# A decoder layer on one core: 3 of 8 pairs of k-tiles of the second SwiGLU's up-projections as 2x2 Strassen products

## The chip, the core and the metric

The kernel runs on one core of one Trainium2 chip. A core has a matrix engine (TensorE, PE in the rows), a vector engine (VectorE, DVE), a scalar engine (ScalarE, ACT), GpSimd (POOL) and SyncE (SP), which here issues the DMAs. Each engine works through its own list of instructions in order and waits at semaphores for the others. SBUF holds operands; products of PE go to PSUM, eight banks of 128 x 512 float32. The metric is the device time of one execution in microseconds (us); lower is better.

## What is computed

One layer with 256 tokens and a model width of 2048. This change concerns the second half-step alone, with `D_FF` = 5632:

```python
def swiglu(x, w1, w3, w2):
    return (jax.nn.silu(x @ w1) * (x @ w3)) @ w2

def reference(x, ...):
    h = x
    h = h + 0.5 * swiglu(rmsnorm(h, ffn1_norm[l]), ffn1_w1[l], ffn1_w3[l], ffn1_w2[l])
    ...                                             # attention and S5 mixers
    h = h + jnp.concatenate([a, s], axis=-1) @ w_out[l]
    h = h + 0.5 * swiglu(rmsnorm(h, ffn2_norm[l]), ffn2_w1[l], ffn2_w3[l], ffn2_w2[l])
    return rmsnorm(h, final_norm)
```

All is float32 and is compared as such. The kernel gets float32 accuracy from PE by splitting each operand into a high part (rounded to the type `fp32r`) and a low part, and by three passes for each product: high x high, high x low, low x high.

## The kernel before

**Tiles.** Tokens are two tiles of 128 (`NT` = 2, index `tt` or `t`), the 2048 channels are 16 k-tiles of 128, taken in 8 pairs. `Norm.cols` (L213) transposes four k-tiles of h on PE into two PSUM banks of the tag "tp" and splits them into `xh` and `xl`, the left operands of all later products; it is called once for each 512 columns of h at the end of the output projection, and `Norm.rstd` then works out the row scale in small DVE instructions.

**Half-step.** `ffn` (L248) goes over 11 chunks of 512 columns. For each, `gemm_rows` (L165) makes x @ w1 for both token tiles into two banks of the tag "mm", ACT takes Silu (L298), `gemm_rows` makes x @ w3 into two more, and DVE multiplies (L302). The gates are transposed (L313, into "tp" banks) and split into the left operand of the product with w2. That product, `down`, is delayed by one chunk: half of the previous chunk's `down` runs between a chunk's up-projections and its transposes, the other half behind the transposes; the first chunk has none before it. Its results are added into h by DVE (L258).

**Weights.** `wload` (L145) has SP load two k-tiles x 512 columns (512 KB) into one of five `raw` slots. `wtiles` (L153) splits each load: `whi` by ACT (L123), `wlo` by DVE (L124), each 128x1024, into one of three slots. A slot is free again when PE's last pass that reads it is done. Each such weight pair serves 2 k-tiles x 2 token tiles x 3 passes = 12 instructions of PE (L176 to L178).

**PSUM.** Tag "mm" has four banks, "tp" two (transposes), "sd" two (the S5 and attention parts, unused in the half-steps).

**Order.** The framework's scheduler sets each engine's list from program order and priorities: the splits of weights are raised by 50 places (`tc.high_priority(offset=50)`), so they stand ahead of other work on ACT and DVE. All other tiles come from one pool of 48 slots of 2 KB, `work`, called wk in rows.

## Time and profile before

| | before |
|---|---|
| median of three runs (lowest to highest) | 1852.6 us (1851.58 to 1853.11) |
| the profiled execution: its own time | 1852.75 us |
| its span, first to last instruction | 1850.2 us |
| PE busy | 1826.3 us, 99% |
| DVE busy | 1196.9 us, 65% |
| ACT busy | 834.2 us, 45% |
| GpSimd busy | 14.7 us |
| loaded from memory | 337.16 MB |
| granted PE clock, mean share of full speed | 0.999 |

Busy times count an instruction from its start to its end; consecutive instructions of an engine overlap somewhat, so starts in a timeline tell more of the pace than durations. Rows of the kernel before carry its line numbers; rows of the order below marked "now" carry those of the changed kernel, where `split` is L127 (ACT) and L128 (DVE).

### The profile page before, as it was taken

What the parts mean: (1) busy time and instruction counts of PE and PEld (TensorE: products, weight loads), DVE (VectorE), ACT (ScalarE), POOL (GpSimd) and SP (SyncE); (2) the same over time, 40 slices, a digit from 0 to 9 for tenths busy, and PEclk for the clock granted to TensorE, in tenths of its full rate; (3) what the DMA queues carried; (4) which work ended last, traced back from release to release, by engine and by line L of the source; (5) the groups of instructions that cost most, each with busy time, mean ns of one, the idle gap of its engine ahead of it and who ended that gap; (6) DMA issues with size and microseconds to landing.
All of it is one profiled execution on the core that took longest, in us unless ns stands there. A gap on an engine that the chain in (4) does not pass through costs nothing.

```text
span 1850.2 us, 24247 instructions
## 1 busy us (share of the span) xinstructions
PE 1826.3 (99%) x9365; PEld 1530.0 (83%) x9365; DVE 1196.9 (65%) x1636; ACT 834.2 (45%) x1081; POOL 14.7 (1%) x32
## 2 busy tenths in 40 slices
PE   8999999999999999999999999999999999999997
PEld 6888888888888888999987788888888888888886
DVE  5477667787887456789876565556555556555656
ACT  6444444434444444555437654443444444444444
POOL 0000000000000000000000000000000000000002
PEclk9999999999999999999999999999999999999999
DMA  7676666665666665654663467666666666666663
GB/s 241 188 210 193 188 188 189 187 177 176 182 198 190 193 187 190 170 149 141 183 211 113 128 180 215 189 188 192 193 189 188 193 192 189 188 193 193 188 194 130
DMA packets 193286, 340.84 MB, mean 184 GB/s; under 512 B 21034, under 2 KB 30868, under 8 KB 193172
## 3 DMA queue, kind: packets, MB, share of 16 engines
q1 hardware_dynamic: 193172, 339.31, 61.4%
q8 instruction: 73, 1.20, 0.3%
q14 instruction: 41, 0.34, 0.0%
HBM read 337.16 MB, written 2.11 MB: 183 GB/s over the span
## 4 chain that ended last, share of the span: by engine, by line
PE 52%; DVE 3%; issue 1%; DMA 1%; ACT 0%; ACTq 0%; SPq 0%; DVEq 0%
PE mm L176 14%; PE mm L178 14%; PE mm L177 14%; PE mm L187 1%; PE mm L188 1%; PE mm L189 1%; PE sd L634 1%; DVE wlo L124 1%; PE tp L798 1%; PE sd L822 1%; PE tp L313 1%; DVE wk L646 0%; PE tp L661 0%; DMA raw<-in_w_in_dram 0%; PE tp L819 0%
## 5 line engine op out<-in xcount | busy, mean ns | idle before, releaser
L124 DVE SCALAR_TENSOR_TENSOR wlo<-raw,whi 128x1024 fp32r<-128x1024 f32 (+1 forms) x620 | 759.1, 1225 | 577.2 <-ACT whi L123 576.1
L123 ACT ACTIVATE whi<-raw 128x1024 fp32r<-128x1024 f32 (+1 forms) x620 | 658.0, 1061 | 922.1 <-PE mm L178 814.5
L176 PE MATMUL mm<-whi,xh 128*128 128x512 f32 x1536 | 601.4, 392 | 2.0 <-ACT whi L123 2.0
L177 PE MATMUL mm<-wlo,xh 128*128 128x512 f32 x1536 | 600.1, 391 | 0.0
L178 PE MATMUL mm<-whi,xl 128*128 128x512 f32 x1536 | 599.8, 391 | 0.0
L176 PEld LDWEIGHTS mm<-whi,xh 128*128 128x128 f32 x1536 | 288.7, 188 | 62.0 <-ACT whi L123 2.4
L177 PEld LDWEIGHTS mm<-wlo,xh 128*128 128x128 f32 x1536 | 288.8, 188 | 60.2 <-DVE wlo L124 1.1
L178 PEld LDWEIGHTS mm<-whi,xl 128*128 128x128 f32 x1536 | 288.6, 188 | 59.5 <-DVE xl L124 0.4
L176 PE MATMUL mm<-whi,wk 128*128 128x512 f32 x688 | 270.3, 393 | 0.0
L178 PE MATMUL mm<-whi,wk 128*128 128x512 f32 x688 | 268.4, 390 | 0.0
L177 PE MATMUL mm<-wlo,wk 128*128 128x512 f32 x688 | 268.0, 390 | 0.0
L178 PEld LDWEIGHTS mm<-whi,wk 128*128 128x128 f32 x688 | 129.1, 188 | 27.1
L176 PEld LDWEIGHTS mm<-whi,wk 128*128 128x128 f32 x688 | 129.2, 188 | 26.6 <-issue 0.6
L177 PEld LDWEIGHTS mm<-wlo,wk 128*128 128x128 f32 x688 | 129.3, 188 | 26.0
L258 DVE SCALAR_TENSOR_TENSOR h<-mm,h 128x512 f32<-128x512 f32 x176 | 113.5, 683 | 2.8 <-PE mm L270 2.1
L187 PE MATMUL mm<-xh,whi 128*128 128x256 f32 x384 | 112.7, 294 | 0.9 <-DVE wk L882 0.9
L188 PE MATMUL mm<-xh,wlo 128*128 128x256 f32 x384 | 108.8, 283 | 0.0
L189 PE MATMUL mm<-xl,whi 128*128 128x256 f32 x384 | 108.8, 283 | 0.0
L187 PEld LDWEIGHTS mm<-xh,whi 128*128 128x128 f32 x384 | 73.4, 191 | 2.8 <-issue 1.2
L188 PEld LDWEIGHTS mm<-xh,wlo 128*128 128x128 f32 x384 | 73.4, 191 | 0.7 <-issue 0.2
L189 PEld LDWEIGHTS mm<-xl,whi 128*128 128x128 f32 x384 | 73.3, 191 | 0.4 <-issue 0.4
L298 ACT ACTIVATE wk<-mm,rstd 128x512 f32<-128x512 f32 x44 | 30.0, 681 | 20.0 <-PE mm L178 20.0
(246 smaller groups left out, 999.7 us busy)
## 6 DMA issues: line engine op xcount, KB each, us to landing
raw<-in_ffn_w_dram SPq DMA_DIRECT2D x528, 512.0 KB, 3.7
raw<-in_w_in_dram SPq DMA_DIRECT2D x48, 512.0 KB, 3.7
raw<-in_w_out_dram SPq DMA_DIRECT2D x32, 512.0 KB, 3.6
raw<-in_w_in_dram SPq DMA_DIRECT2D x8, 536.0 KB, 4.1
raw<-in_glu_w_dram SPq DMA_DIRECT2D x8, 512.0 KB, 4.7
h<-in_x_dram SPq DMA_DIRECT2D x4, 512.0 KB, 8.1
raw<-in_cmp_w_k_dram SPq DMA_DIRECT2D x4, 512.0 KB, 4.5
raw<-in_cmp_w_v_dram SPq DMA_DIRECT2D x4, 512.0 KB, 6.8
```

The costliest lines, as they stand in the source:

```text
L123: S.activation(hi, src, AF.Copy if isinstance(scale, float) else AF.Identity, scale=scale)
L124: V.scalar_tensor_tensor(lo, src, scale, hi.bitcast(F32), op0=ALU.mult, op1=ALU.subtract)
L176: PE.matmul(o, xh[:, t], hi[:, i, :n], start=kt == k0, stop=False)
L177: PE.matmul(o, xh[:, t], lo[:, i, :n], start=False, stop=False)
L178: PE.matmul(o, xl[:, t], hi[:, i, :n], start=False, stop=kt == k1 - 1)
L187: PE.matmul(o, wh, xh, start=kt == 0 and q % 2 == 0, stop=False, skip_group_check=True)
L188: PE.matmul(o, wl, xh, start=False, stop=False, skip_group_check=True)
L189: PE.matmul(o, wh, xl, start=False, stop=last, skip_group_check=True)
L258: V.scalar_tensor_tensor(o, p, 0.5, o, op0=ALU.mult, op1=ALU.add)
L298: S.activation(sl, ps1[tt], AF.Silu, scale=rstd[:, tt:tt + 1])
L313: PE.transpose(ps[:, k, tt * 128:tt * 128 + 128], gates[tt][:, f:f + 128], ident)
L634: PE.matmul(ps[:, hf * 256:hf * 256 + 256], s5.bt[i // 2][ri][:, 2 * (i % 2) + hf, :], up[:, hf].rearrange("p a c -> p (a c)"), start=True ...
```

## The change

In the second half-step alone, w1 and w3 of a chunk are treated as one right operand. For a pair of k-tiles the product is then 2x2 tiles (2 token tiles x 2 k-tiles) by 2x2 tiles (2 k-tiles x {w1, w3}), eight tile products with three passes each. For pairs 1, 3 and 5 (`WINO`) it is made by Strassen's method in Winograd's form, from seven products of sums:

- The four sums of left tiles are made once, in `Norm.combine` at the end of the output projection, and kept.
- The four sums of weight tiles are made for each chunk by DVE from the raw weights (L318), and each sum is split by ACT and DVE into `work` tiles, as is the second k-tile of w3.
- The seven products go to banks of their own: m1, m5, m6, m7 (the four "mm" banks), m2 and m3 ("tp"), m4 and e ("sd"). The three converted pairs accumulate in the same banks. The five other pairs keep eight products, which accumulate straight into m2, m3, m4 and e, the banks that end up as the four results.
- After pair 5, ACT and DVE begin the recombination (L335 to L339), and after pair 7 they add the rest and make the gates.

The body of the loop in `ffn` calls `up_wino` in place of the two `gemm_rows`; `down`, the transposes and the pools stay.

```diff
+WINO = (1, 3, 5)
...
+        def combine(self, pair, ps, scales):
+            y, s = work([128, 2, T]), work([128, 4, 128])
+            for k in range(2):
+                S.activation(y[:, k, :], ps[:, k, :], AF.Identity, scale=scales[k])
+            a11, a21, a12, a22 = (y[:, k, t * 128:t * 128 + 128] for k in range(2) for t in range(NT))
+            V.tensor_tensor(s[:, 0, :], a21, a22, ALU.subtract)
+            V.tensor_tensor(s[:, 2, :], a11, a21, ALU.subtract)
+            V.tensor_tensor(s[:, 1, :], s[:, 0, :], a11, ALU.subtract)
+            V.tensor_tensor(s[:, 3, :], a12, s[:, 1, :], ALU.add)
+            sh, sl = work([128, 4, 128], F32R), work([128, 4, 128], F32R)
+            split(sh, sl, s)
+            self.wino[pair] = sh, sl
...
+        def up_wino(c):
+            m1, m5, m6, m7 = (mm_tile() for _ in range(4))
+            m2, m3 = tp_tile(), tp_tile()
+            m4, e = sd_tile(), sd_tile()
...
+            for p in range(KT // 2):
+                raw1, raw3 = (wload(w[p * 256:p * 256 + 256, f], 512)[:, :, :512] for w in (w1, w3))
+                end = p == KT // 2 - 1
+                if p not in wino:
+                    with tc.high_priority(offset=50):
+                        ws = wpair(raw1), wpair(raw3)
+                    for k in range(2):
+                        for (hi, lo), os in zip(ws, ((m2, m4), (m3, e))):
+                            for t, o in enumerate(os):
+                                passes(o, *pure(k, 2 * p + k, t), hi[:, k, :], lo[:, k, :], end and k == 1)
+                    continue
+                done_ = p == max(wino)
+                with tc.high_priority(offset=50):
+                    hi, lo = wpair(raw1)
+                    b22 = work([128, 512], F32R), work([128, 512], F32R)
+                    split(*b22, raw3[:, 1, :])
+                    sums = []
+                    for a, b in ((raw1[:, 0, :], raw3[:, 0, :]), (0, raw3[:, 1, :]), (raw3[:, 0, :], raw3[:, 1, :]), (1, raw1[:, 1, :])):
+                        s = work([128, 512])
+                        V.tensor_tensor(s, sums[a] if isinstance(a, int) else a, b, ALU.add)
+                        sums.append(s)
+                    sw = []
+                    for s in sums:
+                        sw.append((work([128, 512], F32R), work([128, 512], F32R)))
+                        split(*sw[-1], s)
+                ah, al = xs.wino[p]
+                left = [(ah[:, i, :], al[:, i, :]) for i in range(4)]
+                passes(m1, *pure(0, 2 * p, 0), hi[:, 0, :], lo[:, 0, :], done_)
+                passes(m2, *pure(1, 2 * p + 1, 0), hi[:, 1, :], lo[:, 1, :], False)
+                passes(m3, *left[3], *b22, False)
+                passes(m5, *left[0], *sw[0], done_)
+                passes(m6, *left[1], *sw[1], done_)
+                passes(m7, *left[2], *sw[2], done_)
+                passes(m4, *pure(1, 2 * p + 1, 1), *sw[3], False)
+                if done_:
+                    u1, u2, u3, v, w = (work([128, 512]) for _ in range(5))
+                    S.activation(u1, m1, AF.Copy)
+                    V.tensor_tensor(u2, m6, u1, ALU.add)
+                    V.tensor_tensor(u3, m7, u2, ALU.add)
+                    V.tensor_tensor(v, m5, u2, ALU.subtract)
+                    V.tensor_tensor(w, m5, u3, ALU.subtract)
+            gates = []
+            for t, (a, ua, b, ub) in enumerate(((m2, u1, m3, v), (m4, u3, e, w))):
+                V.tensor_tensor(ua, a, ua, ALU.add)
+                sl = work([128, 512])
+                S.activation(sl, ua, AF.Silu, scale=rstd[:, t:t + 1])
+                V.tensor_tensor(ub, b, ub, ALU.add)
+                V.scalar_tensor_tensor(sl, ub, rstd[:, t:t + 1], sl, op0=ALU.mult, op1=ALU.mult)
+                gates.append(sl)
+            return gates
...
-                n2.cols(n)
+                n2.cols(n, WINO)
...
-    ffn(ffn2_w1[0], ffn2_w3[0], ffn2_w2[0], n2, n2.rstd(), finish, by_tokens=True)
+    ffn(ffn2_w1[0], ffn2_w3[0], ffn2_w2[0], n2, n2.rstd(), finish, by_tokens=True, wino=WINO)
```

Three places show what the change does to the lists of instructions. The names in rows are tiles (wlo and whi are parts of weights, wk is any `work` tile, mm, tp and sd are PSUM banks, cst holds the identity for transposes), the number behind a name tells instances apart, and the brackets at the end say on which engine's or DMA queue's semaphore an instruction waits.

DVE in the middle of a chunk, before:

```order
L124 SCALAR_TENSOR_TENSOR wlo_11894<-raw_11891,whi_11893 128x1024 [waits DMAHW4_49,Activation_49]
L124 SCALAR_TENSOR_TENSOR wlo_11912<-raw_11909,whi_11911 128x1024 [waits DMAHW5_49,Activation_49]
L124 SCALAR_TENSOR_TENSOR wlo_11930<-raw_11927,whi_11929 128x1024 [waits DMAHW6_49,Activation_49]
L124 SCALAR_TENSOR_TENSOR wlo_11948<-raw_11945,whi_11947 128x1024 [waits DMAHW7_49,Activation_49]
L124 SCALAR_TENSOR_TENSOR wlo_11966<-raw_11963,whi_11965 128x1024 [waits DMAHW0_49,Activation_49]
L124 SCALAR_TENSOR_TENSOR wlo_11984<-raw_11981,whi_11983 128x1024 [waits DMAHW1_49,Activation_49]
```

DVE in the middle of a chunk, now, at pair 3 (raw_12200 is w1, raw_12202 is w3):

```order
L128 SCALAR_TENSOR_TENSOR wk_12209<-raw_12202,wk_12208 128x512 [waits DMAHW1_49,Activation_49]
L128 SCALAR_TENSOR_TENSOR wlo_12205<-raw_12200,whi_12204 128x1024 [waits DMAHW0_49,Activation_49]
L318 TENSOR_TENSOR wk_12212<-raw_12200,raw_12202 128x512
L318 TENSOR_TENSOR wk_12214<-wk_12212,raw_12202 128x512 [waits DVE_49]
L318 TENSOR_TENSOR wk_12216<-raw_12202 128x512
L318 TENSOR_TENSOR wk_12218<-wk_12214,raw_12200 128x512 [waits DVE_49]
L128 SCALAR_TENSOR_TENSOR wk_12221<-wk_12212,wk_12220 128x512 [waits Activation_49]
L128 SCALAR_TENSOR_TENSOR wk_12225<-wk_12214,wk_12224 128x512 [waits Activation_49]
L128 SCALAR_TENSOR_TENSOR wk_12229<-wk_12216,wk_12228 128x512 [waits Activation_49]
L128 SCALAR_TENSOR_TENSOR wk_12233<-wk_12218,wk_12232 128x512 [waits Activation_49]
L128 SCALAR_TENSOR_TENSOR wlo_12262<-raw_12257,whi_12261 128x1024 [waits DMAHW2_49,Activation_49]
L128 SCALAR_TENSOR_TENSOR wk_12302<-raw_12295,wk_12301 128x512 [waits DMAHW5_49,Activation_49]
```

Where there were only low parts of loads, there are now, for one pair, the low part of half of w3, that of w1, four sums and the four low parts of the sums.

PE at the start of the first chunk, right behind the output projection, before (L218 are the last transposes of h):

```order
L176 MATMUL mm_9959<-whi_9963,xh_9605 128x512 [waits Activation_49]
L177 MATMUL mm_9959<-wlo_9964,xh_9605 128x512 [waits DVE_49]
L218 MATMUL tp_9907<-cst_73,h_74 128x128 [waits DVE_49]
L218 MATMUL tp_9916<-cst_73,h_74 128x128 [waits PE_49]
L178 MATMUL mm_9959<-whi_9963,xl_9606 128x512
L176 MATMUL mm_9960<-whi_9963,xh_9605 128x512
L218 MATMUL tp_9907<-cst_73,h_74 128x128 [waits DVE_49]
L218 MATMUL tp_9907<-cst_73,h_74 128x128 x2
L218 MATMUL tp_9916<-cst_73,h_74 128x128 x3
L177 MATMUL mm_9960<-wlo_9964,xh_9605 128x512
L178 MATMUL mm_9960<-whi_9963,xl_9606 128x512
```

PE there, now, from the passes that stand behind the same transposes (tp_9943 and tp_9952) on:

```order
L286 MATMUL sd_10001<-wlo_10008,xh_9605 128x512
L287 MATMUL sd_10001<-whi_10007,xl_9606 128x512
L284 MATMUL sd_10002<-whi_10011,xh_9605 128x512
L286 MATMUL sd_10002<-wlo_10012,xh_9605 128x512
L287 MATMUL sd_10002<-whi_10011,xl_9606 128x512
L284 MATMUL mm_9995<-whi_10043,xh_9605 128x512 [waits Activation_49]
L286 MATMUL mm_9995<-wlo_10044,xh_9605 128x512 [waits DVE_49]
L287 MATMUL mm_9995<-whi_10043,xl_9606 128x512
L284 MATMUL tp_9999<-whi_10007,xh_9605 128x512 [waits DVE_49,PE_49]
L286 MATMUL tp_9999<-wlo_10008,xh_9605 128x512
L287 MATMUL tp_9999<-whi_10007,xl_9606 128x512
L284 MATMUL tp_10000<-whi_10011,xh_9605 128x512 [waits DVE_49,PE_49]
```

Before, the products went to "mm" banks and nothing there waited for the split of the transposes; now passes into sd and into m1 come first, and then the "tp" banks are needed, with a wait for DVE.

PE between the first and the second chunk, before (L313 are the transposes of the gates):

```order
L313 MATMUL tp_10257<-cst_73,wk_10105 128x128 [waits DVE_49]
L313 MATMUL tp_10266<-cst_73,wk_10105 128x128 [waits PE_49]
L178 MATMUL mm_10275<-whi_10279,xl_9606 128x512
L176 MATMUL mm_10276<-whi_10279,xh_9605 128x512
L313 MATMUL tp_10257<-cst_73,wk_10107 128x128 [waits DVE_49]
L313 MATMUL tp_10257<-cst_73,wk_10105 128x128
L313 MATMUL tp_10257<-cst_73,wk_10107 128x128
L313 MATMUL tp_10266<-cst_73,wk_10107 128x128
L313 MATMUL tp_10266<-cst_73,wk_10105 128x128
L313 MATMUL tp_10266<-cst_73,wk_10107 128x128
L177 MATMUL mm_10276<-wlo_10280,xh_9605 128x512
```

PE there, now (L414 are the transposes of the gates):

```order
L284 MATMUL mm_10392<-whi_10440,xh_9605 128x512 [waits Activation_49]
L286 MATMUL mm_10392<-wlo_10441,xh_9605 128x512 [waits DVE_49]
L287 MATMUL mm_10392<-whi_10440,xl_9606 128x512
L414 MATMUL tp_10374<-cst_73,wk_10370 128x128 [waits DVE_49]
L414 MATMUL tp_10374<-cst_73,wk_10365 128x128
L414 MATMUL tp_10374<-cst_73,wk_10370 128x128
L414 MATMUL tp_10383<-cst_73,wk_10370 128x128
L414 MATMUL tp_10383<-cst_73,wk_10365 128x128
L414 MATMUL tp_10383<-cst_73,wk_10370 128x128
L284 MATMUL tp_10396<-whi_10404,xh_9605 128x512 [waits DVE_49]
L286 MATMUL tp_10396<-wlo_10405,xh_9605 128x512
L287 MATMUL tp_10396<-whi_10404,xl_9606 128x512
```

The transposes were mixed into the second chunk's first passes and went on into "mm" banks; now passes of the second chunk stand ahead of them and between them, and behind them come passes into the "tp" banks, which wait for DVE.

## Rows read from the trace of the kernel before

**Rows 1.** The page: PE busy; the chain that ended last, by line.

```profile
PE 1826.3 (99%) x9365; PEld 1530.0 (83%) x9365; DVE 1196.9 (65%) x1636; ACT 834.2 (45%) x1081; POOL 14.7 (1%) x32
...
PE mm L176 14%; PE mm L178 14%; PE mm L177 14%; PE mm L187 1%; PE mm L188 1%; PE mm L189 1%; PE sd L634 1%; DVE wlo L124 1%; PE tp L798 1%; PE sd L822 1%; PE tp L313 1%; DVE wk L646 0%; PE tp L661 0%; DMA raw<-in_w_in_dram 0%; PE tp L819 0%
```

**Rows 2.** Windows (second half-step; a chunk): busy us of engines, PEclk, DMA share, GB/s.

```profile
1113.00:1841.00 728.00, 727.84 (x3256) 602.78 (x3253) 408.29 (x425) 311.69 (x335) 8.95 (x7) 1.00 0.64 188
...
1244.34:1310.55 66.21, 66.21 (x297) 54.88 (x296) 36.74 (x37) 27.70 (x29) 0.00 (x0) 1.00 0.65 191
```

**Rows 3.** Timeline of PE in a chunk: start us, duration us, instruction.

```profile
1250.26 0.39 PE L176 MATMUL mm<-whi,xh 128*128 128x512 f32 x1
1250.49 0.39 PE L177 MATMUL mm<-wlo,xh 128*128 128x512 f32 x1
```

**Rows 4.** Timeline of DVE where it works without a pause.

```profile
858.63 0.68 DVE L653 TENSOR_TENSOR wk<-wk 128x512 f32<-128x512 f32 x1
859.23 1.22 DVE L124 SCALAR_TENSOR_TENSOR wlo<-raw,whi 128x1024 fp32r<-128x1024 f32 x1
860.37 0.68 DVE L654 TENSOR_TENSOR xs<-wk 128x512 f32<-128x512 f32 x1
```

**Rows 5.** Groups by shape: busy us, mean ns | idle before.

```profile
L258 DVE SCALAR_TENSOR_TENSOR h<-mm,h 128x512 f32<-128x512 f32 x176 | 113.5, 683 | 2.8 <-PE mm L270 2.1 <-PE mm L178 0.7
...
L302 DVE SCALAR_TENSOR_TENSOR wk<-mm,rstd,wk 128x512 f32<-128x512 f32 x44 | 30.9, 743 | 0.0
L298 ACT ACTIVATE wk<-mm,rstd 128x512 f32<-128x512 f32 x44 | 30.0, 681 | 20.0 <-PE mm L178 20.0
```

**Rows 6.** Timeline near the end: low parts of 128x512, and GpSimd beside them.

```profile
1826.04 2.56 POOL L954 TENSOR_TENSOR wk<-h,wk 128x512 f32<-128x512 f32 x2 [851.13 <-DVE h L258]
...
1827.83 3.12 DVE L124 SCALAR_TENSOR_TENSOR wk<-raw,wk 128x512 fp32r<-128x512 f32 x4 [1.33 <-ACT wk L123]
```

**Rows 7.** Timeline of ACT: conversions of 128x1024 and 128x512.

```profile
1245.02 1.06 ACT L123 ACTIVATE whi<-raw 128x1024 fp32r<-128x1024 f32 x1
1245.99 0.67 ACT L298 ACTIVATE wk<-mm,rstd 128x512 f32<-128x512 f32 x1
...
1278.64 1.07 ACT L123 ACTIVATE wk<-tp 128x512 fp32r<-128x512 f32 x2
```

**Rows 8.** Timeline: a slot's last pass, then ACT and DVE refill it.

```profile
1155.59 0.39 PE L178 MATMUL mm<-whi,xl 128*128 128x512 f32 x1
...
1156.02 1.06 ACT L123 ACTIVATE whi<-raw 128x1024 fp32r<-128x1024 f32 x1 [1.66 <-PE mm L178]
...
1157.11 1.23 DVE L124 SCALAR_TENSOR_TENSOR wlo<-raw,whi 128x1024 fp32r<-128x1024 f32 x1 [0.17 <-ACT whi L123]
```

**Rows 9.** The page, DMA issues: KB each, median us to landing.

```profile
raw<-in_ffn_w_dram SPq DMA_DIRECT2D x528, 512.0 KB, 3.7
```

**Rows 10.** Timelines of PE, ACT and DVE at the end of the output projection.

```profile
1112.53 0.82 PE L218 MATMUL tp<-cst,h 128*128 128x128 f32 x6
...
1113.11 0.82 ACT L123 ACTIVATE xh<-tp,par 128x256 fp32r<-128x256 f32 x2
1113.82 0.63 ACT L208 ACTIVATE wk<-h 128x512 f32<-128x512 f32 x1
...
1119.07 0.16 DVE L242 TENSOR_TENSOR nt<-nt,ms 128x2 f32<-128x2 f32 x1
1119.27 0.17 DVE L243 TENSOR_SCALAR nt<-nt 128x2 f32<-128x2 f32 x1
```

**Rows 11.** Timeline between the first and the second chunk of the second half-step.

```profile
1157.61 1.09 ACT L123 ACTIVATE wk<-tp 128x512 fp32r<-128x512 f32 x2 [0.53 <-PE tp L313]
...
1158.25 1.28 DVE L124 SCALAR_TENSOR_TENSOR wk<-tp,wk 128x512 fp32r<-128x512 f32 x2
```

**Rows 12.** Timeline of PE in its first passes, at the low clock.

```profile
12.73 0.63 PE L178 MATMUL mm<-whi,xl 128*128 128x512 f32 x1
13.16 0.63 PE L177 MATMUL mm<-wlo,xh 128*128 128x512 f32 x1
```

More of the change, by code (lines that the diff above doesn't have):

```diff
@@ L203, in __init__ @@
             self.x = []
+            self.wino = {}
         def square(self, n, tts=(0, 1)):
@@ L208, in square, with cols @@
                 S.activation(junk, h[:, tt, n * 512:(n + 1) * 512], AF.Square, accum_out=self.ssq[:, tt, n:n + 1])
-        def cols(self, n):
+        def combine(self, pair, ps, scales):
[10 more added lines that the diff above has]
+            self.wino[pair] = sh, sl
+        def cols(self, n, wino=()):
             xh = xp.tile([128, 4, T], F32R, name="xh", tag="xh")
@@ L221, in cols @@
                     split(xh[:, 2 * kp + k, :], xl[:, 2 * kp + k, :], ps[:, k, :], par[:, g:g + 1])
+                if 2 * n + kp in wino:
+                    g = self.gain * 16 + 4 * n + 2 * kp
+                    self.combine(2 * n + kp, ps, [par[:, g + k:g + k + 1] for k in range(2)])
             self.x.append((xh, xl))
@@ L245, in rstd, with ffn, passes, pure @@
             return y
-    def ffn(w1, w3, w2, xs, rstd, done, by_tokens=False):
+    def ffn(w1, w3, w2, xs, rstd, done, by_tokens=False, wino=()):
         last = FF // 512 - 1
+        def up_wino(c):
+            m1, m5, m6, m7 = (mm_tile() for _ in range(4))
+            m2, m3 = tp_tile(), tp_tile()
+            m4, e = sd_tile(), sd_tile()
+            begun = set()
+            f = slice(c * 512, c * 512 + 512)
+            def passes(o, xh, xl, wh, wl, stop):
+                PE.matmul(o, xh, wh, start=id(o) not in begun, stop=False)
+                begun.add(id(o))
+                PE.matmul(o, xh, wl, start=False, stop=False)
+                PE.matmul(o, xl, wh, start=False, stop=stop)
+            def pure(k, kt, t):
+                xh, xl = xs(kt)
+                return xh[:, t * 128:t * 128 + 128], xl[:, t * 128:t * 128 + 128]
+            def wpair(raw):
+                hi, lo = (wp.tile([128, WROW], F32R, name=k, tag=k)[:, :1024].rearrange("p (k n) -> p k n", k=2)
+                          for k in ("whi", "wlo"))
+                split(hi, lo, raw)
+                return hi, lo
+            for p in range(KT // 2):
[48 more added lines that the diff above has]
+            return gates
@@ L292, in ffn @@
         for c in range(FF // 512 + 1):
-            if c < FF // 512:
+            if c < FF // 512 and wino:
+                gates = up_wino(c)
+            elif c < FF // 512:
                 ps1 = gemm_rows(xs, w1, c * 512, 512)
```

## The prediction

> **What bounds the kernel now.** I read the page first: the matrix engine (PE) is busy for 99% of the span and the chain that ended last runs mostly through its multiplications [rows 1]. Then the table of windows: in the second half-step (1113 to 1841 us) PE is busy for 727.8 of 728 us at the full clock of 2.4 GHz, and one chunk of 512 columns takes 66.21 us, of which the vector engine (DVE) works 36.7 and the scalar engine (ACT) 27.7 [rows 2]. Busy alone proves little here, so next the timeline of PE: starts lie 0.2267 us apart, without a gap [rows 3]. A chunk has 288 multiplications (8 pairs x 24, and 96 for the product with w2): 288 x 0.2267 = 65.3, and 0.9 for 8 transposes. So PE's count of instructions is the time of this stage, and every other engine has room.
>
> **What is taken away.** A converted pair has seven products of three passes, 21 instead of 24, of the same shape. 3 pairs x 11 chunks x 3 = 99 instructions, 99 x 0.2267 = **22.4 us** if PE still never waits. The new chunk would be 279 x 0.2267 + 0.9 = 64.2 us. The order of the built program confirms 183 passes per chunk for w1 and w3, against 192.
>
> **What DVE gets.** Back to back, a 128x512 instruction of DVE starts 0.60 us after the one before, and a 128x1024 one takes 1.14 [rows 4]. A plain pair costs 2 x 1.14 = 2.3. A converted one costs 1.14 (w1), 0.60 (half of w3), 4 x 0.60 (sums) and 4 x 0.60 (their low parts): 6.5. The recombination adds 8 x 0.60 = 4.8 a chunk. In all a chunk is 21 x 1.14 + 17 x 0.60 + 12 x 0.60 + 8 x 0.60 + 2 x 0.65 + 8 x 0.60 = 52.2 of 64.2 us. The upper bound takes whole durations: 1.23, 0.69, 0.74 and 0.68 [rows 4, 5], and for a low part 0.78, from the slowest four in a row in this trace [rows 6]: 59.8 of 64.2. ACT gets 15 conversions of 128x512 for 3 of 128x1024: 21 x 0.97 + 18 x 0.54 + 2 x 0.68 [rows 5, 7], about 31. So no engine overtakes PE on average, at either end.
>
> On this the Trainium skill speaks otherwise: "VectorE: DVE Perf Modes", section "The DRAIN you can't avoid", says that the next instruction does not start until the pipe is empty. The starts 0.60 apart of instructions that last 0.69 [rows 4] say that it does; by the page's rule DVE's sum would be near 58 instead of 52.2, still under 64.2.
>
> **A steady chunk (the third to the eleventh).** Averages don't settle it, since DVE's work comes in lumps and only three whi/wlo slots exist. Time 0 is PE's first pass of pair 0; pairs begin at 0, 5.4, 10.2, 15.6, 20.4, 25.8, 30.6, 36.1. DVE's order there: at 0.7 it has the last add into h, and all of pair 0 and most of pair 1 is done. Freeing a slot costs 0.43 to ACT, 1.09 more to DVE, 1.23 for the low part [rows 8], so a slot freed by a pass that starts at t gives a weight at t + 2.75. Pair 2's w1 (slot free at 3.9) is there at 6.6, wanted at 10.2; the last product of pair 1 stands behind it and is done at 7.2, wanted at 9.5. Pair 3: sums to 12.4, low parts to 14.8, wanted from 17.7. Pair 5: sums to 22, low parts to 24.5, wanted from 27.9. Only pair 7's w3 is close: its slot is freed by pair 6's 18th pass (starts 34.5), there at 37.2, wanted at 37.6. Weights land 3.7 us after issue [rows 9] and are issued 4 us or more ahead of that. The chain of gates after pair 7 hides behind the 48 passes (10.9 us) of the product with w2. So I take 0; at DVE's upper bound pair 5 is just in time, and I allow 0.5 a chunk, 4.5 in all.
>
> **Where there is no such cover.** The new code takes all eight PSUM banks, among them the two "tp" banks that transposes use, and the first chunk has no product with w2 beside it.
>
> *Start of the first chunk.* Before, PE goes on with w1 into free banks while the last transposes of h (end of the output projection) are split: no gap [rows 10]. Now it has 15 passes and 8 transposes that need no tp bank (3.4 + 0.9 = 4.3 us), then waits until ACT and DVE have read the transposes: those end at about 2.8, then two xh, two squares and two xh on ACT (0.36 and 0.63 each, to 5.6) and a low part: 5.8. Stall 1.5. Then DVE runs fourteen small instructions for rstd, 0.20 apart [rows 10], from 7.1 to 9.9, ahead of pair 2's w1, whose low part is there at 11.2 while PE wants it at 9.7: 1.5. From there DVE leads PE by less than 1 us: 0.5 at pair 3's w1, 0.9 at pair 4's w1, whose load waits for a raw slot that DVE frees at 13.6. Sum **4.4**; bounds 1.5 (only the bank) and 9 (DVE at its slowest prices over 30 us of this lockstep).
>
> *First chunk to second.* After the last pass DVE still adds, multiplies and splits, PE transposes, ACT and DVE convert [rows 11], and only then are the tp banks free: from order and rows at 6.0 after the last pass, while PE has 15 passes and 8 transposes, 4.3. About **2.0** with the hand-overs; bounds 0 and 3.5.
>
> *Second chunk.* DVE leads by 0 to 1 us: **0.5**, bounds 0 and 3.
>
> *Left operands.* combine() adds 2 x 0.4 and 0.54 on ACT, 4 x 0.25 (an estimate between 0.20 and 0.60 by size) and 0.60 on DVE to three column blocks of 10.9 us in which DVE is little over half busy: 0, at most 1.
>
> **Sum.** -22.4 + 4.4 + 2.0 + 0.5 = -15.5. The profiled execution took 1852.75 us, its span 1850.2 and 2.55 around it; it stands 0.15 above the median of the three runs, 1852.6. 1852.75 - 15.5 = **1837.3 us**. Low end: -22.4 + 1.5 gives 1831.9, rounded to 1831. High end: with 9, 3.5, 3, 4.5 and 1 it is 1851; all of these together are unlikely, and I end at 1848.
>
> **Rivals.**
> *DVE is nearer to its upper bound* (each new instruction costs its whole duration, or is slowed by ACT reading the same tiles). For it: four 128x512 low parts from raw tiles in a row took 0.78 each [rows 6]; against it: GpSimd worked beside the first of those, and it has nothing to do here. Then the first two chunks cost 12 to 15 and the steady ones up to 0.5: 1842 to 1850. By the Trainium skill's page on the DRAIN only the lockstep of the first chunk grows, some 45 instructions x 0.09 = 4 us, so 1841.
> *Slower: sum, conversion and low part go hand in hand.* If DVE stands at each low part until ACT has just converted its sum, a low part costs 0.63 + 0.69 + 0.07 instead of 0.60, 3.2 a converted pair, 9.6 a chunk. DVE would then need about 36 us up to the end of pair 5 against PE's 30.6; after its lead some 3 us a chunk are left: 9 x 3 = 27, and 1864. It decides from 1.4 us a chunk on ((22.4 - 6.9)/11). Against it: all four sums precede the four low parts in DVE's order, and ACT (0.54 each) keeps ahead of 0.60; for it: ACT's own queue is in order, and a conversion that waits for a whi slot holds back the sums behind it.
> *The first chunks cost nothing*, since the scheduler already moved passes between pairs: 1831.
> *The clock falls.* In rows PE at the low clock shows passes 0.43 apart [rows 12] against 0.2267. The Trainium skill, "TensorE: Matmul & The Clock Gate", section "A second HAM failure mode: psum-queue depth-cycling", has matmuls that cycle through banks lose the clock. If 2013 passes ran at 0.43 it would be 400 us more; but PE changes banks every three passes already, at clock 1.00 [rows 2, 3]: 1 in 100.
>
> **Chances.** Forecast (1833 to 1842) 0.66; DVE near its bound 0.15, two thirds of it still faster by over 0.2%; free start 0.08; slower 0.10; clock 0.01. 0.2% (3.7 us) is about what a measurement can tell from no change. Faster 0.66 + 0.08 + 0.10 = 0.84, same 0.05, slower 0.11. The range 1831 to 1848 holds the forecast, the free start and about half of the rival: 0.82.
>
> **What would show it.** PE idle near zero from the third chunk on, chunks 64.2 us apart; PE idle of 4 to 5 us in the first chunk, first named tp banks, then DVE's wlo; about 2 at the second's start; DVE busy (durations counted) 55 to 60 us a chunk. Wrong if a steady chunk takes over 64.7, if starts of DVE lie over 0.65 apart, or if ACT's conversions of sums end DVE's waits.

## The result, and the profile after

The changed kernel takes 1838.8 us (median of four runs, 1838.4 to 1839.6) against 1852.9 (four runs, 1851.6 to 1853.2): a ratio of 0.9926, 95% interval 0.9909 to 0.9943. The profiled run took 1839.61, its span 1837.7; it is the slowest of the four.

The page first, the line of the engines that answers to [rows 1]:

```profile
PE 1808.9 (98%) x9266; PEld 1509.9 (82%) x9266; DVE 1391.5 (76%) x2003; ACT 895.9 (49%) x1233; POOL 14.7 (1%) x32
```

9365 - 9266 = 99 instructions of PE are gone and its busy time fell by 17.4 us, but DVE has 194.6 us more. The windows of the second half-step answer to [rows 2] (us, then busy us and instructions of PE, PEld, DVE, ACT, POOL, granted clock, DMA share, GB/s). The first runs from the first pass of the half-step to the wait between the first and the second chunk, the second to just behind the transposes of gates in the second chunk, the third from there to the first of those in the third, and the last two are whole chunks, from one transpose of gates to the next:

```profile
1111.61:1161.29 49.68, 47.16 (x199) 34.97 (x197) 43.48 (x76) 28.75 (x45) 0.00 (x0) 1.00 0.61 195
1161.29:1217.20 55.91, 54.66 (x243) 43.61 (x243) 47.90 (x62) 29.21 (x39) 0.00 (x0) 1.00 0.59 189
1217.20:1281.40 64.20, 63.40 (x280) 51.98 (x278) 52.82 (x67) 32.09 (x41) 0.00 (x0) 1.00 0.62 193
1281.40:1345.53 64.13, 64.13 (x288) 53.19 (x287) 54.06 (x69) 33.01 (x41) 0.00 (x0) 1.00 0.64 197
1345.53:1409.67 64.14, 64.14 (x289) 53.19 (x288) 54.09 (x69) 33.01 (x41) 0.00 (x0) 1.00 0.63 197
```

From the fourth window on PE is busy for the whole window, at the full clock, and a chunk takes 64.13 instead of 66.21. Before that PE stands idle in every window. What ended those waits, in the table of PE's waits over the whole half-step (us in total, times, longest):

```profile
PE tp L286 <- DVE wlo L128: 1.2, 2, 0.8
PE tp L284 <- DVE wk L128: 1.1, 1, 1.1
PE tp L284 <- DVE xl L128: 0.9, 1, 0.9
PE sd L284 <- DVE wk L345: 0.6, 1, 0.6
PE mm L284 <- ACT wk L127: 0.3, 1, 0.3
PE sd L284 <- ACT wk L127: 0.2, 1, 0.2
```

That is only 4.3 us. More is lost than the table holds: a pass behind a wait starts late itself, and the next is 0.11 later than its pitch, and short pauses have no row. So I measure losses from starts. From the first pass of the output projection to the last pass of the kernel it is 1840.45 - 996.80 = 843.65 us before and 1827.94 - 997.29 = 830.65 now, 13.0 less, where 99 passes are worth 22.4: **9.4 us lost**, against 6.9 in the sum. (The work ahead of the output projection, which the change does not touch, ends anywhere from 995.7 to 998.0 in the profiles of this study. That is the scatter of a single run, and measuring from 996 on leaves it out.) In starts against the pitch of 0.2267, about 5 of it lie in the first chunk, about 3 between the first and the second, 0.5 in the second, 1.0 in the third (one load that came late, as the last section but two shows), nothing of note behind.

Three places in rows. The start of the first chunk, PE, ACT and DVE (start us, duration, instruction, in brackets the idle time and what ended it), answering to [rows 10]:

```profile
1110.11 0.82 ACT L219 ACTIVATE wk<-tp,par 128x256 f32<-128x256 f32 x2
1114.83 0.63 ACT L213 ACTIVATE wk<-h 128x512 f32<-128x512 f32 x1
1115.45 0.63 ACT L213 ACTIVATE wk<-h 128x512 f32<-128x512 f32 x1
1116.06 0.83 ACT L127 ACTIVATE xh<-tp,par 128x256 fp32r<-128x256 f32 x2
1116.57 0.88 DVE L128 SCALAR_TENSOR_TENSOR xl<-tp,par,xh 128x256 fp32r<-128x256 f32 x2 [0.58 <-ACT xh L127]
1117.19 0.47 PE L284 MATMUL tp<-whi,xh 128*128 128x512 f32 x1 [0.94 <-DVE xl L128]
1118.15 0.17 DVE L255 TENSOR_REDUCE ms<-ssq 128x2 f32<-128x8 f32 x1 [0.71 <-ACT wk L213]
```

PE waits for the tp bank, the bank for the split of h, the split for ACT, and ACT has two squares (L213) ahead of it. L219 is combine() for the column block ahead. The gap between first and second chunk, answering to [rows 11]:

```profile
1161.29 0.47 PE L284 MATMUL sd<-whi,xh 128*128 128x512 f32 x1 [0.57 <-DVE wk L345]
1164.05 0.87 PE L414 MATMUL tp<-cst,wk 128*128 128x128 f32 x6
1166.01 0.50 PE L284 MATMUL tp<-whi,xh 128*128 128x512 f32 x1 [1.08 <-DVE wk L128]
```

And DVE in a steady chunk, answering to [rows 4]:

```profile
1291.12 0.68 DVE L318 TENSOR_TENSOR wk<-raw 128x512 f32<-128x512 f32 x1
1291.84 0.69 DVE L318 TENSOR_TENSOR wk<-wk,raw 128x512 f32<-128x512 f32 x1
1292.44 1.22 DVE L128 SCALAR_TENSOR_TENSOR wlo<-raw,whi 128x1024 fp32r<-128x1024 f32 x1
1293.58 0.69 DVE L318 TENSOR_TENSOR wk<-raw 128x512 f32<-128x512 f32 x1
1294.18 0.69 DVE L318 TENSOR_TENSOR wk<-wk,raw 128x512 f32<-128x512 f32 x1
```

The starts are 0.60 apart behind a 128x512 instruction and 1.14 behind a 128x1024 one, as in the kernel before, also for the new sums, but for one: the second sum reads what the first has just written, and where it stands right behind it, it starts 0.72 later (1291.12 to 1291.84; so in 31 of the 33 converted pairs).

### The profile page after: what moved, and what is told of

It is laid out like the page before. It is cut to its first block, busy times and chain, and to the rows that moved or that the text cites. A ratio compares the mean times of both kernels' runs of the same rounds, so it can differ in the third digit from the quotient of the medians.

```text
span 1837.7 us, 24559 instructions
## 1 busy us (share of the span) xinstructions
PE 1808.9 (98%) x9266; PEld 1509.9 (82%) x9266; DVE 1391.5 (76%) x2003; ACT 895.9 (49%) x1233; POOL 14.7 (1%) x32
## 5 line engine op out<-in xcount | busy, mean ns | idle before, releaser
L180 PE MATMUL mm<-whi,xh 128*128 128x512 f32 x832 | 327.6, 394 | 2.0 <-ACT whi L127 2.0
L181 PE MATMUL mm<-wlo,xh 128*128 128x512 f32 x832 | 326.2, 392 | 0.0
L182 PE MATMUL mm<-whi,xl 128*128 128x512 f32 x832 | 325.7, 392 | 0.0
L180 PEld LDWEIGHTS mm<-whi,xh 128*128 128x128 f32 x832 | 156.6, 188 | 34.7 <-ACT whi L127 2.4
L181 PEld LDWEIGHTS mm<-wlo,xh 128*128 128x128 f32 x832 | 156.7, 188 | 33.0 <-DVE wlo L128 1.1
L182 PEld LDWEIGHTS mm<-whi,xl 128*128 128x128 f32 x832 | 156.6, 188 | 32.0 <-DVE xl L128 0.4
L182 PEld LDWEIGHTS mm<-whi,wk 128*128 128x128 f32 x688 | 129.1, 188 | 26.8
L127 ACT ACTIVATE wk<-wk 128x512 fp32r<-128x512 f32 x139 | 83.5, 626 | 55.5 <-DVE wk L318 49.7
L284 PE MATMUL tp<-whi,xh 128*128 128x512 f32 x253 | 98.7, 391 | 2.2 <-DVE wk L128 1.1
L286 PE MATMUL tp<-wlo,xh 128*128 128x512 f32 x253 | 98.9, 392 | 1.2 <-DVE wlo L128 1.2
L287 PE MATMUL tp<-whi,xl 128*128 128x512 f32 x253 | 98.4, 390 | 0.0
```

The lines of the kernel that those rows point to most:

```text
L127: S.activation(hi, src, AF.Copy if isinstance(scale, float) else AF.Identity, scale=scale)
L180: PE.matmul(o, xh[:, t], hi[:, i, :n], start=kt == k0, stop=False)
L181: PE.matmul(o, xh[:, t], lo[:, i, :n], start=False, stop=False)
L182: PE.matmul(o, xl[:, t], hi[:, i, :n], start=False, stop=kt == k1 - 1)
L284: PE.matmul(o, xh, wh, start=id(o) not in begun, stop=False)
L286: PE.matmul(o, xh, wl, start=False, stop=False)
```

## The experiments

Each kernel is the changed kernel with one edit, but for the two under "Put together", which join several, and "five pairs, two sums", which edits the version with five pairs. The table gives, beside the median, the time from the first pass of the output projection to the last pass in the profile, the passes that fall away against the kernel before, and what is lost: 843.65 - 0.2267 x passes, taken from that time. The last two columns belong to the one profiled run; it stood 2.8 us above the median with double sums, 3.3 with five pairs and two sums, and about 1 at most elsewhere. The kernel before took 1852.1 to 1852.4 beside the experiments.

| kernel | median us | passes less | us in that stretch | lost us |
|---|---|---|---|---|
| before | 1852.9 | 0 | 843.65 | 0 |
| changed | 1838.8 | 99 | 830.65 | 9.4 |
| one pair | 1847.7 | 33 | 839.04 | 2.9 |
| eight products | 1859.2 | 0 | 850.92 | 7.3 |
| double sums | 1862.3 | 99 | 856.46 | 35.2 |
| four pairs | 1839.0 | 132 | 829.53 | 15.8 |
| banks swapped | 1834.7 | 99 | 826.45 | 5.2 |
| rstd later | 1836.7 | 99 | 828.47 | 7.3 |
| plain first chunk | 1834.5 | 90 | 826.42 | 3.2 |
| five pairs | 1891.1 | 165 | 883.41 | 77.2 |
| first chunk with two pairs | 1832.1 | 96 | 823.84 | 1.9 |
| four pairs, plain first chunk | 1829.4 | 117 | 820.70 | 3.6 |
| no combine | 1833.6 | 99 | 826.11 | 4.9 |
| five pairs, two sums | 1839.8 | 165 | 833.08 | 26.8 |

### Does the gain come from the passes?

**Eight products** (e2):

```diff
+                passes(m7, *left[2], *sw[2], False)
                 passes(m7, *left[2], *sw[2], done_)
```

> A converted pair gets three passes back (the product into m7 is added twice, so the output is another), all else stays. Theory: PE's count of passes is the whole gain; 99 x 0.2267 = 22.4 come back, less 1 to 2 of first-chunk stalls that the extra passes cover: 1859 to 1861, steady chunk 66.2. Rival: part of the gain comes from the other order or the eight banks, or the steady chunk is already held by DVE: under 1857, steady chunk under 66.0.

1859.2 us, ratio to before 1.0041 (1.0026 to 1.0056). A steady chunk, in the windows:

```profile
1416.97:1483.15 66.18, 66.18 (x298) 54.90 (x296) 53.91 (x69) 33.13 (x41) 0.00 (x0) 1.00 0.59 191
```

Nine passes more, and the chunk is 2.05 us longer (9 x 0.2267 = 2.04). With the eight banks, the order and all of DVE's work in place but the passes back, the stretch is 7.3 us longer than before, the cost of the arrangement alone. The theory holds; the rival falls.

### What does DVE's work cost, and how much more does it bear?

**Double sums** (e3), **four pairs** (e4), **five pairs** (e8):

```diff
                         V.tensor_tensor(s, sums[a] if isinstance(a, int) else a, b, ALU.add)
+                        V.tensor_tensor(s, s, b, ALU.add)
```

```diff
-WINO = (1, 3, 5)
+WINO = (1, 3, 5, 6)
```

```diff
-WINO = (1, 3, 5)
+WINO = (1, 2, 3, 5, 6)
```

> Each of the four sums of a converted pair is followed by one more 128x512 add into itself (12 more DVE instructions a chunk; the output is another). Theory (a DVE instruction costs its start pitch, 0.60): DVE's busy time of 54.1 a chunk becomes 61.3 of 64.1, and since the lumps are larger at pairs 5 and 7 a steady chunk loses 0 to 1; first three chunks lose 8 to 14 more: 1847 to 1858. Rival (an instruction costs its whole duration, 0.69): 59.8 + 8.2 = 68 a chunk, DVE sets the time: 1838.8 + 9 x 3.9 + 10 = 1884.

> Pair 6 is converted too (1, 3, 5, 6). Theory: another 33 passes go, -7.5; steady chunk 62.1, DVE at 58.3 by start pitches; the first chunks lose 1 to 2 more: 1832 to 1834. Rival (DVE at whole durations, 59.8 + 4.9 = 64.7 a chunk): steady chunk 64.7, no gain: 1839 to 1845. Between them: pairs 5 and 6 in a row are too much for DVE's lead, about 1 us a chunk lost: 1841.

> Pairs 1, 2, 3, 5 and 6 are converted. A pair takes 3 passes from a chunk, so a steady chunk has 273 passes and 8 transposes, 62.8 (the 62.1 told for four pairs was a slip, 276 passes are 63.5, and 63.7 was measured). DVE's busy time, 54.1 with three pairs and 58.3 with four, would be 62.6. Theory (DVE becomes the bound): steady chunk 64 to 66, DVE busy over 95% of it, first three chunks 6 to 10 worse: 1845 to 1860. Rival (PE's count still sets the time): steady chunk 63.0, 1834 to 1840.

A chunk of each in the windows, double sums, then four pairs, then five:

```profile
1422.72:1488.97 66.25, 65.48 (x289) 52.58 (x287) 60.86 (x81) 32.11 (x41) 0.00 (x0) 1.00 0.61 190
```

```profile
1411.37:1475.05 63.68, 63.68 (x286) 52.55 (x285) 57.98 (x77) 34.66 (x45) 0.00 (x0) 1.00 0.61 197
```

```profile
1436.46:1504.66 68.20, 65.75 (x282) 52.90 (x281) 61.98 (x85) 36.31 (x49) 0.00 (x0) 0.97 0.56 185
1418.00:1426.00 8.00, 6.75 (x20) 5.03 (x21) 6.81 (x10) 3.11 (x7) 0.00 (x0) 0.79 0.66 244
```

Twelve more adds raise DVE's busy time by 60.86 - 54.09 = 6.8 us, 0.57 each, so a DVE instruction in a run costs about its start pitch, and the rival of whole durations (1884 us) falls. But the kernel took 1862.3, above the 1847 to 1858 told: PE loses 2.1 us in a steady chunk although DVE has 5.4 us to spare in it. Four pairs lose only 0.2 a steady chunk (63.68 against 276 x 0.2267 + 0.92 = 63.49); the kernel is still no faster than with three, 1839.0, since 6.4 us more are lost, 5.3 of it in the first chunk and the gap behind it. Five pairs are slower than the kernel before, by 2.1% (ratio 1.0208, 1.0193 to 1.0224), and further than I had told. A chunk takes 68.2 where PE's count is 62.8. One of its places, ACT first, then PE:

```profile
1417.27 1.06 ACT L127 ACTIVATE whi<-raw 128x1024 fp32r<-128x1024 f32 x1 [3.33 <-DVE wk L318]
1418.23 2.17 ACT L127 ACTIVATE wk<-wk 128x512 fp32r<-128x512 f32 x4
1418.90 1.02 PE L284 MATMUL mm<-wk 128*128 128x512 f32 x2 [1.67 <-ACT wk L127]
1420.24 0.55 PE L286 MATMUL mm<-wk 128*128 128x512 f32 x1 [0.32 <-DVE wk L128]
1420.58 0.63 PE L287 MATMUL mm<-wk 128*128 128x512 f32 x1
1421.01 0.63 PE L284 MATMUL mm<-wk 128*128 128x512 f32 x1
```

The first product of a sum waits for ACT's conversion, the next for DVE's low part, and behind them passes start 0.43 apart: the clock, 0.79 over these 8 us in the window above, has fallen. DVE had begun the first of these sums at 1414.23; ACT converted all four only from 1418.23, since a conversion of loaded weights stood ahead in its list and itself waited 3.33.

**Five pairs, two sums** (e12), to see whether that is DVE's lateness:

```diff
+                        if isinstance(a, int):
+                            sums.append(b)
+                            continue
                         s = work([128, 512])
-                        V.tensor_tensor(s, sums[a] if isinstance(a, int) else a, b, ALU.add)
+                        V.tensor_tensor(s, a, b, ALU.add)
```

> Five pairs with two of the four sums of each pair left out (raw tiles are converted in their place, so the output is another); every pass of PE stays as with five pairs. 10 DVE instructions a chunk fall away, 6.0 us: DVE at about 57 of 63. Theory (the five-pair version is slow because DVE is late, and PE's clock only falls behind those waits): chunks near 63.0, clock 1.00 in steady chunks, 165 x 0.2267 = 37.4 less 9 to 13 in the first three chunks: 1824 to 1828. Rival (the short passes into many banks, ACT's 25 conversions or the loads hold it): chunks stay over 65, 1855 or more.

1839.8 us: 51 less than five pairs, so it is DVE's sums that hold five pairs, and the clock is back at 1.00 with two of the four gone. Whether the sums do it by the time that they take on DVE or by holding up ACT's list, as above, this run doesn't tell apart. And it isn't 1824 to 1828:

```profile
1411.92:1476.51 64.59, 63.52 (x282) 51.91 (x281) 56.16 (x75) 36.00 (x49) 0.00 (x0) 1.00 0.61 196
```

DVE is now less busy than with four pairs and PE still waits 0.8 for its low part (this chunk is 1.8 over its count of 62.8; chunks four to eleven lose 0.5 to 1.9, 1.3 in the mean). The share of busy time does not tell this; 87% loses more here than 91% did with four pairs. What differs is that pairs 1, 2, 3 and 5, 6 stand in a row: a converted pair takes PE 4.8 us and DVE 6.5 (5.3 with two sums), so DVE falls back at each and has no plain pair to make it up. That reading fits both, but no run with the five pairs placed otherwise was made.

### Where do the 9.4 us go?

The same loss by place, in starts against the pitch of 0.2267, and of 0.115 for a transpose (us): the passes of the first chunk's up-projections, the 40 passes behind them with their transposes, the rest of the second chunk, all later. The sums come within 0.5 of the last column above; below nothing means that transposes stand closer together than before.

| kernel | first chunk | gap behind it | second chunk | later |
|---|---|---|---|---|
| changed | 5.2 | 3.1 | 0.5 | 1.0 |
| one pair | 0.6 | 2.5 | 0.1 | -0.1 |
| no combine | 1.4 | 3.1 | 0.5 | 0.0 |
| banks swapped | 3.4 | 0.4 | 2.2 | -0.3 |
| rstd later | 4.4 | 3.1 | 0.4 | -0.3 |
| plain first chunk | 1.1 | 1.8 | 0.7 | 0.0 |
| first chunk with two pairs | 0.5 | 0.3 | 1.8 | -0.3 |

**One pair** (e1):

```diff
-WINO = (1, 3, 5)
+WINO = (3,)
```

> Only pair 3 of each chunk is converted, so 33 passes fall away instead of 99: -7.5 us. Theory: most of the loss (9.4 us in the trace of the changed kernel) belongs to the eight banks and the two tp banks among them, not to the converted pairs: about 1.9 at the start of the first chunk, 3.2 between first and second chunk (each 0.7 more than now, since the three passes of m1 no longer stand ahead), 1 for a low part that comes late: 1852.9 - 7.5 + 6.1 = 1851.5. Rival: the loss goes with the number of converted pairs, a third of 9.4: 1852.9 - 7.5 + 3.1 = 1848.5. Steady chunks 65.5 us in both.

1847.7 us, lost 2.9: my theory (banks alone, 1851.5) is wrong, and the rival's number (a third of the loss) came, but not its picture. The loss doesn't shrink evenly with the pairs: the gap keeps 2.5 of 3.1, and the first chunk falls from 5.2 to 0.6. The eight banks are in use here too, and PE comes to the tp bank without a wait of note; PE's waits are

```profile
PE tp L284 <- DVE wk L128: 0.6, 1, 0.6
PE sd L284 <- DVE wk L345: 0.6, 1, 0.6
```

Both lie between first and second chunk. So at the start it is not the bank by itself; something that comes with more pairs makes it late. Two kinds of DVE's and ACT's work come with pairs, the sums and combine().

**No combine** (e11). The left sums are left out; plain tiles stand in for them:

```diff
...
-            y, s = work([128, 2, T]), work([128, 4, 128])
-            for k in range(2):
-                S.activation(y[:, k, :], ps[:, k, :], AF.Identity, scale=scales[k])
...
-            split(sh, sl, s)
...
```

> The left sums of combine() are left out (plain tiles of the same size stand in their place, so the output is another); all else as in the changed kernel. Theory (its 2 ACT and 4 to 5 DVE instructions per block, above all the last block's, push the split of the last transposes of h back): the wait for the tp bank at the start, 1.1 to 1.2, shrinks by about half, and the first chunk's later waits with it: 0.5 to 1.5 less, 1837.3 to 1838.3. Rival (combine costs nothing, the bank alone does): 1838.8, first wait 1.1.

1833.6 us, 5.2 less, far over the 0.5 to 1.5 told. The first wait is gone altogether. ACT and PE at the start there (the first pass starts at 1110.27, in the changed kernel at 1111.61):

```profile
1112.80 0.62 ACT L213 ACTIVATE wk<-h 128x512 f32<-128x512 f32 x1
1113.42 0.83 ACT L127 ACTIVATE xh<-tp,par 128x256 fp32r<-128x256 f32 x2
1114.24 0.39 PE L276 MATMUL mm<-wlo,xh 128*128 128x512 f32 x1
1114.55 0.47 PE L274 MATMUL tp<-whi,xh 128*128 128x512 f32 x1
```

The last xh begins 3.15 us behind the first pass, against 1116.06 - 1111.61 = 4.45; two squares fewer are queued around it on ACT, since without combine() those of the column block ahead were done earlier, at 1099.52 and 1100.13. With one pair, whose combine() belongs to an earlier block, they are early too (1101.76 and 1102.38), which fits that there PE didn't wait at the start. With the first wait go the later ones of the first chunk, but for one of 0.2 in the table of waits; between first and second chunk they stay (0.6 and 1.1). So work that I had costed at nothing because three column blocks cover it stands for 3.8 of the 5.2 us lost in the first chunk: it shifts ACT's and DVE's other work into the stretch where PE has no cover. Whether it is the time of combine()'s instructions or the place in ACT's list that the squares get behind them, no run tells apart. The whole loss fell by 4.5, from 9.4 to 4.9, since the third chunk's late load isn't there either.

**Banks swapped** (e5), in the first two chunks only:

```diff
-            m1, m5, m6, m7 = (mm_tile() for _ in range(4))
-            m2, m3 = tp_tile(), tp_tile()
+            if c < 2:
+                m6, m7, m2, m3 = (mm_tile() for _ in range(4))
+                if c == 1:
+                    m2, m3, m6, m7 = m6, m7, m2, m3
+                m1, m5 = tp_tile(), tp_tile()
...
```

> First two chunks only: m2 and m3, which are used first, go to mm banks and m1 and m5, which are used from pair 1 on, to the tp banks; of the product with w2 of chunk 0 the first column block accumulates in tp banks. Theory: the waits for the tp banks at the start (1.2) and between first and second chunk (2.5 with what follows) go, and little comes in their place: 1838.8 - 3.3 = 1835.5. Rival: at the start DVE's low parts are the limit behind the bank, so PE only waits for pair 2's low part instead, 1.2 longer than now; only the second wait goes: 1837.0.

1834.7 us (told 1835.5). Of the waits for the tp banks none is left, nor that for the sd banks in the gap; the longest are now:

```profile
PE mm L290 <- ACT whi L127: 0.5, 1, 0.5
PE mm L292 <- DVE wlo L128: 0.5, 2, 0.2
PE sd L290 <- ACT whi L127: 0.2, 1, 0.2
```

So combine() makes the tp banks late, and the waits for those banks are part of what it costs: with the banks swapped the first chunk still loses 3.4, without combine() 1.4. Each of the two edits alone takes away 4 to 5 us, 1.0 of it the third chunk's late load. For the rest it is not the same loss: the swapped banks take 2.7 from the gap and 1.8 from the first chunk and bring 1.7 in the second; no combine() takes 3.8 from the first chunk and nothing from the gap. No run has both edits.

**rstd later** (e6):

```diff
...
             for p in range(KT // 2):
+                if p == 3 and callable(rstd):
+                    rstd = rstd()
...
```

> The fourteen small DVE instructions of rstd are written behind pair 2 of the first chunk instead of ahead of pair 0. Theory (they hold back pair 2's low part): the waits at 1121.2 and 1122.1, together 1.0, go: 1837.8. Rival (the load or ACT's conversion of the same weights would be late anyway, ACT being free of the squares only at 1118.1): the same wait is then put down to ACT, and the time stays at 1838.8.

1836.7 us, and neither reading is tested, since the edit did not reach what it was aimed at. DVE at pair 2's low part (wlo), with ACT's conversion of the same weights, in the changed kernel, and then here:

```profile
1119.61 1.06 ACT L127 ACTIVATE whi<-raw 128x1024 fp32r<-128x1024 f32 x1 [1.49 <-issue]
1120.73 0.16 DVE L264 TENSOR_TENSOR nt<-nt,ms 128x2 f32<-128x2 f32 x1
1120.82 1.23 DVE L128 SCALAR_TENSOR_TENSOR wlo<-raw,whi 128x1024 fp32r<-128x1024 f32 x1
```

```profile
1119.41 0.16 DVE L264 TENSOR_TENSOR nt<-nt,ms 128x2 f32<-128x2 f32 x1
1119.50 1.23 DVE L128 SCALAR_TENSOR_TENSOR wlo<-raw,whi 128x1024 fp32r<-128x1024 f32 x1
```

The scheduler left the same fourteen small instructions ahead of the low part, and only the last two of rstd come later, so the waits at pair 2 stay to the hundredth (0.29 and 0.64 in starts). The first three rows still answer the question: ACT's conversion ends at 1120.67 and the low part, which needs it, starts at 1120.82, so without the small instructions it could have started 0.15 earlier at most. The rival's cause, ACT, is there beside rstd. What is gone is 0.8 in the first chunk, behind pair 2, where DVE's list has another order, and the 1.0 of the third, the late load.

**Plain first chunk** (e7):

```diff
+            wino = {0: ()}.get(c, WINO)
...
```

> The first chunk keeps all eight products in the same banks and has no sums; the other ten are as before. Nine passes come back: +2.0. Theory (the sums of the first chunk keep DVE just ahead of PE, in lockstep): the waits between 1126 and 1135 go, 2.2, and DVE enters the second chunk with a lead, so that its waits and that of the third (0.7 + 1.1) shrink too: 1837 to 1839. Rival (only the banks and rstd cost anything, DVE's waits are small change): the nine passes are lost: 1840.8.

1834.5 us, better than either told: 2.0 us of passes come back and the loss falls from 9.4 to 3.2. In the first chunk, where no product with w2 gives DVE time, three converted pairs save 2.0 us and cost about 5, first chunk and gap together.

### Put together

**First chunk with two pairs** (e9: e5 and e6, and pairs 3 and 5 in the first chunk) and **four pairs, plain first chunk** (e10: e5 and e6, none in the first chunk, three in the second, four from the third on):

> Three things together: the banks of the first two chunks as in the swapped version (m2 and m3 in mm, m1 and m5 in tp), rstd written behind pair 2, and only pairs 3 and 5 converted in the first chunk. 96 passes fall away, 21.8 us: with no wait left 1852.5 - 21.8 = 1830.7. Theory (DVE's short lead in the first chunk is what is left): 1.0 to 2.5 of waits remain: 1831.7 to 1833.2. Rival (the parts remove the same waits twice): no better than the swapped banks or the plain first chunk alone, 1834.5.

> Four pairs (1, 3, 5, 6) from the third chunk on, three in the second, none in the first, with the swapped banks and rstd written behind pair 2. Passes less: 9 + 9 x 12 = 117, 26.5 us; steady chunks were 0.2 above their count with four pairs, 1.9 in all; first chunks 1 to 2: 1852.5 - 26.5 + 3.4 = 1829.4. Theory (the four-pair version lost its gain in the first two chunks, 8 us of waits there, not in the steady ones): 1828 to 1831. Rival (the steady chunk has no slack left and falls out of step when it starts from another state): steady chunk over 64, 1834 or more.

1832.1 us and 1829.4 (ratio to before 0.9875, 0.986 to 0.9889), both as told. A steady chunk of the second:

```profile
1402.47:1466.11 63.64, 63.64 (x286) 52.55 (x285) 57.92 (x77) 34.66 (x45) 0.00 (x0) 1.00 0.62 199
```

The same four pairs that gained nothing when only WINO was changed give 9.4 us more than the changed kernel, once the first two chunks are started otherwise. Most of that is not the fourth pair's: three pairs with the other start (e9) had 6.7 of it already. And a first chunk with two converted pairs loses no more (0.5) than a plain one (0.5 in e10), once the banks are swapped.

## Why the prediction was right, and where it was not

- **Passes, 22.4 us:** right. A steady chunk takes 64.13 to 64.14 for 64.2, and with the passes put back 66.18.
- **DVE's price:** right, for the sum. The busy time of a steady chunk is 54.1, between 52.2 and 59.8 and near the lower end, though under the 55 to 60 that the prediction names as a sign; twelve adds cost 0.57 each. One of its signs of being wrong, starts over 0.65 apart, is met by the second of the four sums (0.72), which the starts in [rows 4] couldn't show; at three in a chunk it is 0.4 us. By the rule of the DRAIN that the prediction weighs twelve adds would have taken 0.69 each. The prediction left out how the Trainium skill goes on there: in "VectorE: DVE Perf Modes", section "The DRAIN you can't avoid", an instruction that is not held starts earlier, and the trace agrees (starts 0.60 apart).
- **Steady chunks, 0:** right from the fourth on, and pair 7's w3, the place called close, shows no wait. The third lost 1.0, which the sum did not have and the change does not explain. SP's issue of one load and ACT's wait for it, then the same place a chunk later, and last what PE lost in the third:

```profile
1218.64 0.37 SPq L152 DMA_DIRECT2D raw<-in_ffn_w_dram  x1
1225.12 0.63 ACT L127 ACTIVATE wk<-raw 128x512 fp32r<-128x512 f32 x1 [4.16 <-DMA raw<-in_ffn_w_dram]
1283.95 0.37 SPq L152 DMA_DIRECT2D raw<-in_ffn_w_dram  x1
1288.36 0.63 ACT L127 ACTIVATE wk<-raw 128x512 fp32r<-128x512 f32 x1 [2.09 <-DMA raw<-in_ffn_w_dram]
1230.48 0.50 PE L286 MATMUL tp<-wlo,xh 128*128 128x512 f32 x1 [0.80 <-DVE wlo L128]
```

  The load was issued at the same place of the chunk both times (1218.64 and 1283.95, 65.31 apart, as the transposes of gates are), but landed 6.46 us later the first time and 4.39 the second. It is the slowest load of weights in this half-step (median 4.46). Each of the five other profiled runs with these three pairs from the second chunk on loses nothing there, so I put this 1.0 down to the one run, and 8.4 of the 9.4 to the change.
- **Start of the first chunk, 4.4:** 5.2, inside its bounds, and the first two waits came where the prediction put them: 1.2 for the tp bank (told 1.5) and 1.0 at pair 2 (told 1.5). But their causes were put wrongly. At pair 2 ACT's conversion is as late as rstd, to 0.15. And what failed is the last term of the sum, "Left operands: 0, at most 1": without combine() 3.8 of the 5.2 are not lost (e11). The prediction had read the two squares ahead of the last xh out of the new order and so had the wait in its sum, without asking what had put them there. So the size of the start came out and its source didn't, and the expectations of one pair and of no combine, which rested on the source, missed.
- **First chunk to second, 2.0:** 3.1, inside its bounds. The wait for the tp bank was there (1.1); an earlier one was not in the sum, in which the sd banks wait for the last additions into the gates (L345, 0.6).
- **Second chunk, 0.5:** 0.5.
- **Sum:** 6.9 told, 9.4 lost in the profiled run, which took 1839.6, 2.3 above the 1837.3 told; the median, 1838.8, is 1.5 above. No term was told too large and so made up for another.
- **Rivals:** DVE at its upper bound and sums hand in hand did not come with three pairs. With five, part of the second did: DVE's four low parts of a pair still follow each other without a wait (2.49 us for four from 1419.50), but ACT's conversions of the sums stood behind one that waited 3.33, much as the prediction's last sentence on this rival has it, and the kernel is slower than before. The free start (1831) falls with the 8 us lost in the first chunk and the gap. The clock did not fall in the changed kernel, which goes through all eight banks (1.00 in every window above); with five pairs it did, behind waits of PE. That fits what "TensorE: Matmul & The Clock Gate", section "A second HAM failure mode: psum-queue depth-cycling", of the Trainium skill tells of, an engine that idles for short times between groups; the prediction had taken from it the change of banks alone. The rows say that the waits matter, and not the change of banks.

## What to carry to other kernels

Trading passes for vector work pays at the full rate where the vector engine has a stretch of other passes to run ahead in, and not in the first turns of a loop, where it has none; leave the first turn, or its first pairs, plain. Side work that is "covered" is not free if it comes just ahead of such a stretch: look at what it pushes back. And a share of busy time is a poor limit for lumpy work: here 91% lost 0.2 us a chunk in one order, and 87% lost 0.5 to 1.9 in another. And before an edit's time is read, look in its trace whether the instructions stand where the edit was to put them; rstd's did not.

## What was not expected of the hardware

With five pairs, PE waited 1.67 us and, 1.3 us later, some 0.9 in starts; then eight passes or so started 0.43 apart instead of 0.2267, the spacing of the low clock in [rows 12], and the granted clock of 1418 to 1426 was 0.79. In other chunks of the same kernel the same two waits came (1.67 at 1351.89) and the passes behind them stood 0.23 apart. So late operands can cost PE twice, and not every time; what decides it, these runs don't show. It is the smaller part: in the half-step 61 passes stand 0.43 apart, in ten places, some 12 of the 77 us lost.
